# The lower halves of sixteen weight pieces are made by GpSimd and not by VectorE

## The chip, the cores and the metric

The kernel runs on one core of a Trainium2 chip. The metric is the device time of one execution in microseconds (us). The engines of a core work side by side, each through its own list of instructions in a fixed order, and wait for each other through semaphores: TensorE (PE in the profile, PEld for its weight loads), VectorE (DVE), ScalarE (ACT), GpSimd (POOL) and SyncE (SP, which issues most DMAs).

## The reference, cut to what matters

A trunk of two layers over 512 tokens of width 1024 in float32: an RG-LRU block, a gated conv-MLP, an RWKV-7 time-mixing block and a second gated conv-MLP, with an RMS norm ahead of each. The change touches the weights of two of the RWKV block's products:

```
xs_rkv = jnp.stack([h + xx * mix[0], h + xx * mix[1], h + xx * mix[2]])
rkv = jnp.einsum('sbtd,sde->sbte', xs_rkv, w_rkv)
r, k, v = rkv[0], rkv[1], rkv[2]
```

`w_rkv[0]` makes r, `w_rkv[1]` makes k, both 1024 x 1024.

## The kernel before, in words

**Products in three passes.** A float32 product is made of three products of a shorter type. Each operand is split into a higher part `hi`, rounded to that type (F32R), and a lower part `lo = src - hi`; `mm3` (L50) then adds wh*xh, wh*xl and wl*xh in one PSUM bank. In `split` (L92) ScalarE makes `hi` (L94, a CAST in the profile) and VectorE makes `lo` (L97, a TENSOR_TENSOR that reads `src` and `hi` from SBUF).

**Weights stream in pieces.** `plan_weights` (L100) lists all weight pieces of the kernel in the order in which they are used. A piece is 128 partitions x 1024 values, 512 KB. `weights_load` (L161) issues its DMA into a tile `raw`, `weights_split` (L172) makes `wh` and `wl` of it, and `next_weights` (L188) hands out the next piece, with loads 3 pieces ahead and splits 2 (3 in one product) ahead. `raw`, `wh`, `wl` and many other tiles share a ring of 21 buffers (`b4`, L84). k has 8 pieces, r the next 8, then come those of v.

**The stage of the change.** The feed-forward block of the first layer ends at about 540 us of the span. Then come: the small matrices of the decay and the gates (`rwkv_lora_k`, L1036), the k product (blocks 0 to 3 beside that, blocks 4 to 7 in `rwkv_krv`, L1128), the r product, and from `rwkv_chunks` (L1350) the v product with the recurrence. A product is `project_gen` (L197): for an output group of four PSUM banks it takes one piece after the other, the last two together.

**Beside the products** VectorE runs `prepare` (L1162), once for each half of the heads: it scales k and the decay, sums squares through TensorE (`ssq`, L1185; `sst`, L1200), takes reciprocals (tile `n`, L1202 and L1204), which TensorE transposes (`rec`, L1208), VectorE splits (L1211), TensorE spreads (`knb`, L1217) and VectorE multiplies in (L1218). After it `solve` (L1264) inverts 32 x 32 triangles in 31 steps of two instructions each (L1308, L1310) and writes its result XN (L1315), which TensorE's `m1p` (L1334) waits for. The `mix` tiles (L965, L970, L97) are the split operands of r and v.

**GpSimd before** has little to do here: constants (`selk`, `sel`, `n`), the unit matrix X of `solve` (L1303, L1304), the triangle `masks` of the recurrence (L1373, and nine selections at L1380), and small copies (`rts` L1444, `tu` L1447).

**What sets the order.** The program text gives priorities, background work is spread between the products by counts (`background`, L62), and a scheduler of the framework then orders each engine's list by its own estimates, except where `keep_in_program_order` or a dependency fixes it. Once written, an engine's list is strictly in order: an instruction that waits holds all behind it.

Of the kernel before, what the change touches and what calls it, by code (L numbers as in the profile page):

```python
# [7 lines left out]
F32 = mybir.dt.float32  # L8
F32R = mybir.dt.float32r
AF = mybir.ActivationFunctionType  # L10
ALU = mybir.AluOpType
# [33 lines left out]
class Kernel:  # L45
# [43 lines left out]
        t = self.b4(F32R, (2, T), name)  # L89
        return t[:, 0], t[:, 1]  # L90

    def split(self, src, hi, lo, dve=False, pin=False):  # L92

        put = (self.nc.vector.tensor_copy if dve else self.nc.scalar.copy)(hi, src)  # L94
        if pin:
            self.tc.keep_in_program_order(put)
        self.nc.vector.tensor_tensor(lo, src, hi.bitcast(F32), ALU.subtract)  # L97


    def plan_weights(self):  # L100
        I = self.I
        plan = []
        self.quads = []

        def piece(w, r0, c0, k):
            return w[r0 : r0 + k * P, c0 : c0 + D // k].rearrange("(k p) c -> p k c", p=P)

        def add(w, r0, c0, k=2):
            plan.append((piece(w, r0, c0, k), k, False, None))

        def full(w, groups, rows=8):
            for g in groups:
                for k in range(0, rows, 2):
                    add(w, k * P, g * 512)

        def ffn(l):
            up, dn = I["ffn_w_up"][l], I["ffn_w_down"][l]

            def gu(six):


                for n in range(2 * six, 2 * six + 2):
                    self.quads.append(len(plan))
                    a = lambda i, j: piece(up, j * 512, (1 - i) * DFF + n * 256, 4)
                    if n in HALVES:
                        for first, more in (((0, 0), None), ((1, 1), (1, 0)), ((0, 1), None), ((1, 0), (0, 0)), ((1, 1), None)):
                            plan.append((a(*first), 4, True, more and a(*more)))
                    else:
                        for i, j in ((1, 0), (0, 0), (1, 1), (0, 1)):
                            plan.append((a(i, j), 4, False, None))  # L130
                self.quads.append(len(plan))

            def dd(row, n):
                for g in range(2):
                    for k in range(0, n, 2):
                        add(dn, row + k * P, g * 512)

            gu(0)
            for six in range(1, 6):
                gu(six)  # L140
                if six < 5:
                    dd((six - 1) * 512, 4)
            dd(2048, 8)

        full(I["lru_w_in"][0], [2, 3, 0, 1])
        full(I["lru_w_out"][0], [0, 1])
        ffn(0)
        for i in (1, 0):
            full(I["rwkv_w_rkv"][0, i], [0, 1])
        for g in range(4):  # L150
            for k in range(0, 8, 4):
                add(I["rwkv_w_rkv"][0, 2], k * P, g * 256, 4)
        for h in range(2):
            for g in range(4):
                add(I["rwkv_w_out"][0], h * 512, g * 256, 4)
        ffn(1)
        self.plan = plan
        self.loaded, self.splitted = {}, {}
        self.n_load = self.n_split = self.n_used = 0
# [12 lines left out]
    def weights_split(self, upto, pin=False):  # L172
        while self.n_split < min(upto, len(self.plan)):
            i = self.n_split
            if self.plan[i][2]:
                self.n_split += 1
                continue
            self.weights_load(i + 1)
            raw = self.loaded.pop(i)
            k = self.plan[i][1]  # L180
            hi = self.b4(F32R, (k, D // k), f"wh{i}")
            lo = self.b4(F32R, (k, D // k), f"wl{i}")
            for j in range(k) if i == 0 else [slice(0, k)]:
                self.split(raw[:, j], hi[:, j], lo[:, j], pin=pin)
            self.splitted[i] = (hi, lo)
            self.n_split += 1

# [1599 lines left out]
```

## Time and profile before

| | us |
|---|---|
| three runs | 1277.94, 1277.94, 1279.10; median 1277.94 |
| the profiled execution | 1279.1 |
| its span, first to last instruction | 1277.3 |
| VectorE busy in it | 929.2 |
| ScalarE busy in it | 642.8 |
| GpSimd busy in it | 131.1 |

The profiled execution is 1.16 us above the median of the runs; 1.8 us of it lie around the span. TensorE's clock was granted at 0.998 of full speed on average. The profile gives groups of instructions by source line, engine and tiles, the waits between engines, busy time by window, and a timeline in which a row can stand for several instructions of one kind that follow each other (x2, x4); the time of such a row reaches from the start of the first to the end of the last.

### The profile page before, as it was taken

The page shows a single profiled execution, that of the slowest core. Times are in us where ns is not written, and L with a number is a line of the kernel's source. Part 1 is how long each engine was busy: PE and PEld are TensorE (multiplying, and loading weights), DVE is VectorE, ACT ScalarE, POOL GpSimd, SP SyncE. Part 2 cuts the span into 40 slices and gives each one's busy share as a digit, 9 for nine tenths or more (in the row PEclk, how much of TensorE's full clock was granted, in tenths as well). Part 3 has the DMA queues.
Part 4 walks back from the last instruction along what each step waited for, and adds up shares of the span by engine and source line. Part 5 has one row for each costly group of instructions (what it writes and reads, how often), then busy time and mean ns, then how long its engine had stood idle before and what let it go on. Part 6 is the DMA issues. An engine that isn't in the chain of part 4 may idle for free. (4 is left out here: it accounts for less than half of the span.)

```text
span 1277.3 us, 22409 instructions
## 1 busy us (share of the span) xinstructions
PE 1256.0 (98%) x9259; PEld 1067.4 (84%) x9259; DVE 929.2 (73%) x1412; ACT 642.8 (50%) x1006; POOL 131.1 (10%) x206
## 2 busy tenths in 40 slices
PE   9999999999999999999999898999999999999998
PEld 8777888989898989877778797778889898989896
DVE  5998678767676767789999967778776666666654
ACT  6797455434343434559845356545644334343442
POOL 3000001010101010010012145310010101000000
PEclk9999999999999999999999999999999999999999
DMA  7312335445454544413222122122345454545431
GB/s 228 109 53 97 98 119 114 158 106 167 97 175 89 181 83 137 141 57 110 67 75 68 35 63 85 50 94 83 127 88 181 83 182 83 182 83 182 98 133 66
DMA packets 117829, 141.37 MB, mean 111 GB/s; under 512 B 10138, under 2 KB 91748, under 8 KB 117600
## 3 DMA queue, kind: packets, MB, share of 16 engines
q1 hardware_dynamic: 100528, 122.44, 29.9%
q0 software_dynamic: 16624, 16.47, 8.3%
q8 instruction: 72, 1.18, 0.4%
q10 hardware_dynamic: 576, 1.05, 0.2%
q14 instruction: 29, 0.24, 0.1%
HBM read 135.41 MB, written 4.52 MB: 110 GB/s over the span
## 5 line engine op out<-in xcount | busy, mean ns | idle before, releaser
L97 DVE TENSOR_TENSOR wl<-raw,wh 128x1024 fp32r<-128x1024 f32 (+1 forms) x161 | 194.4, 1213 | 123.6 <-ACT wh L94 103.8
L94 ACT CAST wh<-raw 128x1024 fp32r<-128x1024 f32 (+1 forms) x161 | 165.9, 1043 | 179.8 <-PE acc L54 40.7
L54 PE MATMUL accU<-xs,wh 128*128 128x512 f32 x448 | 138.6, 391 | 0.0
L54 PE MATMUL accG<-xs,wh 128*128 128x512 f32 x448 | 138.6, 390 | 0.0
L54 PE MATMUL acc<-hid,wh 128*128 128x512 f32 x384 | 117.9, 389 | 0.0
L748 DVE TENSOR_TENSOR lo<-raw,hi 128x1024 fp32r<-128x1024 f32 x70 | 85.5, 1222 | 39.4 <-PE accU L54 32.0
L747 ACT CAST hi<-raw 128x1024 fp32r<-128x1024 f32 x70 | 73.7, 1054 | 60.4 <-PE accU L54 25.3
L54 PEld LDWEIGHTS accU<-xs,wh 128*128 128x128 f32 x448 | 83.7, 188 | 17.1
L54 PEld LDWEIGHTS accG<-xs,wh 128*128 128x128 f32 x448 | 83.7, 188 | 17.0
L54 PE MATMUL accU<-xs,wl 128*128 128x512 f32 x224 | 87.2, 389 | 0.0
L54 PE MATMUL accG<-xs,wl 128*128 128x512 f32 x224 | 87.2, 389 | 0.0
L54 PE MATMUL accA<-xt,hi 128*128 128x256 f32 x480 | 83.5, 277 | 0.0
L54 PEld LDWEIGHTS acc<-hid,wh 128*128 128x128 f32 x384 | 71.4, 188 | 14.3
L54 PE MATMUL acc<-xs,wh 128*128 128x512 f32 x256 | 80.9, 398 | 0.0
L694 DVE SCALAR_TENSOR_TENSOR cv<-gpad,pv,cv 128x512 f32<-128x512 f32 x96 | 69.1, 747 | 13.1 <-ACT cv L692 12.7
L848 PE MATMUL acc<-wh,hid 128*128 128x512 f32 (+1 forms) x200 | 76.2, 381 | 0.0
L849 PE MATMUL acc<-wl,hid 128*128 128x512 f32 (+1 forms) x200 | 76.1, 381 | 0.0
L847 PE MATMUL acc<-wh,hid 128*128 128x512 f32 (+1 forms) x200 | 76.1, 381 | 0.0
L54 PE MATMUL acc<-hid,wl 128*128 128x512 f32 x192 | 74.3, 389 | 0.0
L168 POOL DMA_DIRECT2D raw<-in_ffn_w_up_dram x20 | 25.7, 1285 | 469.8 <-DVE x L863 166.5
L54 PEld LDWEIGHTS accA<-xt,hi 128*128 128x128 f32 x480 | 72.6, 188 | 0.0
L54 PE MATMUL accA<-xt,lo 128*128 128x256 f32 x240 | 66.3, 276 | 0.0
(411 smaller groups left out, 2938.0 us busy)
## 6 DMA issues: line engine op xcount, KB each, us to landing
raw<-in_ffn_w_up_dram SPq DMA_DIRECT2D x106, 512.0 KB, 3.9
raw<-in_ffn_w_down_dram SPq DMA_DIRECT2D x48, 512.0 KB, 4.0
raw<-in_ffn_w_up_dram POOLq DMA_DIRECT2D x30, 512.0 KB, 5.7
raw<-in_rwkv_w_rkv_dram SPq DMA_DIRECT2D x24, 512.0 KB, 3.8
raw<-in_lru_w_in_dram SPq DMA_DIRECT2D x16, 512.0 KB, 4.0
raw<-in_lru_w_out_dram SPq DMA_DIRECT2D x8, 512.0 KB, 3.8
raw<-in_rwkv_w_out_dram SPq DMA_DIRECT2D x8, 512.0 KB, 3.8
xd<-x SPq DMA_DIRECT2D x8, 256.0 KB, 2.1
```

The lines of the kernel that those rows point to most:

```text
L54: mm = lambda *a, **kw: self.nc.tensor.matmul(ps, *a, skip_group_check=more, **kw)
L94: put = (self.nc.vector.tensor_copy if dve else self.nc.scalar.copy)(hi, src)
L97: self.nc.vector.tensor_tensor(lo, src, hi.bitcast(F32), ALU.subtract)
L168: self.nc.gpsimd.dma_start(raw, more, accum_op=ALU.add)
L694: nc.vector.scalar_tensor_tensor(cv, pair.gp[:, e, j : j + T], cw(j), cv, ALU.mult, ALU.add)
L747: nc.scalar.copy(hi, f[p])
L748: tt(lo, f[p], hi.bitcast(F32), ALU.subtract)
L847: nc.tensor.matmul(ps, hh[:, s], wh[:, k, m], start=kk == 0, stop=False)
L848: nc.tensor.matmul(ps, hl[:, s], wh[:, k, m], start=False, stop=False)
L849: nc.tensor.matmul(ps, hh[:, s], wl[:, k, m], start=False, stop=kk == blocks - 1)
```

## The change

`split` gets a switch `pool`, with which the subtraction for `lo` is issued on GpSimd. `plan_weights` remembers which entries of the plan are the pieces of k and r (`aside`), and `weights_split` sets the switch for them. Sixteen subtractions of 128 x 1024 move; the casts, the loads, the sizes of the tiles and the matmuls stay.

```
-    def split(self, src, hi, lo, dve=False, pin=False):
+    def split(self, src, hi, lo, dve=False, pin=False, pool=False):
...
-        self.nc.vector.tensor_tensor(lo, src, hi.bitcast(F32), ALU.subtract)
+        (self.nc.gpsimd if pool else self.nc.vector).tensor_tensor(lo, src, hi.bitcast(F32), ALU.subtract)
...
         ffn(0)
+        first = len(plan)
         for i in (1, 0):
             full(I["rwkv_w_rkv"][0, i], [0, 1])
+        self.aside = range(first, len(plan))
...
-                self.split(raw[:, j], hi[:, j], lo[:, j], pin=pin)
+                self.split(raw[:, j], hi[:, j], lo[:, j], pin=pin, pool=i in self.aside)
```

Since the scheduler orders the lists anew, other instructions move too. In the changed program the line numbers behind the plan are higher by two (L1204 is L1206 there); the numbers of tiles are the same in both.

GpSimd's list at the end of the stage, before; LT_6284 and X belong to `solve`, tu to the recurrence:

```order
L1303 MEMSET X 128x1024
L1304 AFFINE_SELECT X<-X 128x1024
L1373 MEMSET masks 128x384
L1444 COPY rts<-AR_4906 64x128
L1380 AFFINE_SELECT masks<-masks 64x64 x9
L1444 COPY rts<-AR_4906 64x128 x3
L1409 MEMSET tu 64x256
```

The same place now:

```order
L1306 AFFINE_SELECT X<-X 128x1024
L97 TENSOR_TENSOR wl_5689<-raw_5599,wh_5688 128x1024
L97 TENSOR_TENSOR wl_5695<-raw_5686,wh_5694 128x1024
L97 TENSOR_TENSOR wl_5790<-raw_5692,wh_5789 128x1024
L97 TENSOR_TENSOR wl_5877<-raw_5787,wh_5876 128x1024
L1375 MEMSET masks 128x384
L1446 COPY rts<-AR_4906 64x128
L1382 AFFINE_SELECT masks<-masks 64x64 x9
L1446 COPY rts<-AR_4906 64x128 x3
L97 TENSOR_TENSOR wl_5955<-raw_5874,wh_5954 128x1024
L1411 MEMSET tu 64x256
```

Four pieces of r stand ahead of the masks, and the last piece of r, wl_5955, stands behind the masks, their selections and four copies.

TensorE's list where the last two pieces of r (wh_5876 with wl_5877, and wh_5954 with wl_5955) meet the banks acc_5783 to acc_5786, before:

```order
L54 MATMUL acc_5786<-mix,wh_5876 128x512 x2
L54 MATMUL acc_5786<-mix,wl_5877 128x512
L54 MATMUL acc_5783<-mix,wh_5954 128x512 x2
L54 MATMUL acc_5784<-mix,wh_5954 128x512 x2
L54 MATMUL acc_5785<-mix,wh_5954 128x512 x2
L54 MATMUL acc_5786<-mix,wh_5954 128x512 x2
L54 MATMUL acc_5783<-mix,wl_5955 128x512
L54 MATMUL acc_5783<-mix,wh_5954 128x512 x2
```

And now, from the second half of the knb products on:

```order
L1219 MATMUL knb<-rec,back 128x512 x2
L54 MATMUL acc_5783<-mix,wl_5877 128x512
L1219 MATMUL knb<-rec,back 128x512 x2
L54 MATMUL acc_5783<-mix,wh_5954 128x512 x2
L54 MATMUL acc_5784<-mix,wh_5876 128x512 x2
L54 MATMUL acc_5784<-mix,wl_5877 128x512
L54 MATMUL acc_5783<-mix,wl_5955 128x512
L54 MATMUL acc_5783<-mix,wh_5954 128x512 x2
```

Before, all products with wh_5876 and eight with wh_5954 stood ahead of the first with wl_5955. Now five matmuls stand between the last knb product and the first with wl_5955.

VectorE's list around the second round of reciprocals (tile n_5222; D_5527 and X are the steps of `solve`), before:

```order
L97 TENSOR_TENSOR wl_5877<-raw_5787,wh_5876 128x1024
L1308 TENSOR_TENSOR D_5527<-A,X 128x240
L965 TENSOR_SCALAR mt<-x,om 128x512
L1310 TENSOR_TENSOR X<-X,D_5527 128x20x12
L1202 TENSOR_SCALAR n_5222<-sst 128x4x8
L1308 TENSOR_TENSOR D_5527<-A,X 128x247
L1204 RECIPROCAL n_5222<-n_5222 128x4x8
L1310 TENSOR_TENSOR X<-X,D_5527 128x19x13
L1204 RECIPROCAL n_5222<-n_5222 128x4x8
```

And now:

```order
L1310 TENSOR_TENSOR D_5527<-A,X 128x255
L972 SCALAR_TENSOR_TENSOR mt<-x,pv,mt 128x511
L1312 TENSOR_TENSOR X<-X,D_5527 128x17x15
L1204 TENSOR_SCALAR n_5222<-sst 128x4x8
L1310 TENSOR_TENSOR D_5527<-A,X 128x256
L1206 RECIPROCAL n_5222<-n_5222 128x4x8
L1312 TENSOR_TENSOR X<-X,D_5527 128x16x16
L1206 RECIPROCAL n_5222<-n_5222 128x4x8
```

Three steps of `solve` (D 128x252, 128x255, 128x256 and their updates of X), two instructions of L970 and one of L965 that stood behind the reciprocals stand ahead of them now. Counted over the lists, VectorE has seven pieces fewer from its first L1046 to the end of the first round of reciprocals and is the same there otherwise; six fewer and these nine instructions more from there to the end of the second round; one fewer, and these nine fewer, from there to XN.

## The prediction

> **What bounds the kernel now.** I read the page first, for the engine that is full and for the group that the change touches; then the windows of the stage in which k and r are made; then what TensorE waits for there.
>
> ```profile
> PE 1256.0 (98%) x9259; PEld 1067.4 (84%) x9259; DVE 929.2 (73%) x1412; ACT 642.8 (50%) x1006; POOL 131.1 (10%) x206
> L97 DVE TENSOR_TENSOR wl<-raw,wh 128x1024 fp32r<-128x1024 f32 (+1 forms) x161 | 194.4, 1213 | 123.6 <-ACT wh L94 103.8
> ...
> 576.00:617.00 41.00, 40.12 (x181) 31.22 (x180) 37.96 (x73) 39.31 (x67) 1.00 (x18) 1.00 0.33 99
> 617.00:640.00 23.00, 22.18 (x208) 16.26 (x208) 21.98 (x37) 17.52 (x40) 2.23 (x2) 1.00 0.27 79
> 640.00:672.00 32.00, 31.07 (x138) 23.33 (x139) 31.65 (x69) 13.25 (x21) 4.49 (x14) 1.00 0.22 67
> 672.00:696.00 24.00, 23.25 (x337) 20.91 (x337) 23.55 (x46) 12.38 (x27) 3.53 (x5) 1.00 0.21 67
> ...
> PE m1p L1334 <- DVE XN L1315: 0.7, 1, 0.7
> PE rec L1208 <- DVE n L1204: 0.5, 1, 0.5
> ```
>
> The numbers of a window are its length and then busy PE, PEld, DVE, ACT, POOL. TensorE is full in the whole run, and in this stage VectorE is nearly full too: 37.96 of 41 us, 21.98 of 23, 31.65 of 32, 23.55 of 24. TensorE's idle time here is only 0.88 + 0.82 + 0.93 + 0.75 = 3.38 us. That is all that a lighter VectorE could give back in the stage. The two waits show where VectorE is late already: at the reciprocals (rec) and at the end of the solve (m1p) TensorE waits for it with no slack, so whatever VectorE loses ahead of these points TensorE loses too. GpSimd is nearly idle. The question is whether VectorE gets faster when GpSimd takes the pieces.
>
> **What is taken from VectorE.** The step from a piece to the next instruction:
>
> ```profile
> 584.22 1.20 DVE L97 TENSOR_TENSOR wl<-raw,wh 128x1024 fp32r<-128x1024 f32 x1
> 585.34 1.05 DVE L1107 TENSOR_TENSOR_SCAN AR<-keep,sg 128x128 f32<-128x128 f32 x3
> ...
> 616.12 0.74 DVE L1204 RECIPROCAL n<-n 128x32 f32<-128x32 f32 x2
> ...
> 661.85 0.34 DVE L1204 RECIPROCAL n<-n 128x32 f32<-128x32 f32 x1
> ```
>
> One piece takes 585.34 - 584.22 = 1.12 us out of VectorE's stream. By the lists seven pieces go ahead of the first round of reciprocals, which ends at 616.86 (7 x 1.12 = 7.8 us), and six between it and the end of the second round at 662.19 (6.7 us).
>
> **What a piece costs on GpSimd.** No row shows this subtraction there. The nearest are its product bv, also of two float32 tiles but 512 wide, and its copies:
>
> ```profile
> 740.60 1.04 POOL L1538 TENSOR_TENSOR bv<-x,bon 128x512 f32<-128x512 f32 x1
> 774.15 2.03 POOL L1538 TENSOR_TENSOR bv<-x,bon 128x512 f32<-128x512 f32 x1
> 704.20 0.40 POOL L1447 COPY tu<-x 64x256 f32<-64x256 f32 x1
> 737.55 0.29 POOL L1444 COPY rts<-AR 64x128 f32<-64x128 f32 x1
> 719.04 1.06 POOL L1447 COPY tu<-x 64x256 f32<-64x256 f32 x2 [4.78 <-DVE wl L97]
> ...
> 740.85 0.69 DVE L1431 TENSOR_TENSOR W<-s,masks 128x512 f32<-128x512 f32 x1
> 774.06 1.21 DVE L97 TENSOR_TENSOR wl<-raw,wh 128x1024 fp32r<-128x1024 f32 x1
> 709.99 0.42 DVE L1310 TENSOR_TENSOR X<-X,DA 128x247 f32<-128x247 f32 x1
> 719.23 0.60 DVE L1310 TENSOR_TENSOR X<-X,DA 128x247 f32<-128x247 f32 x1
> ```
>
> bv took 1.04 us at 740.60. Twice the width gives at most 2.08 us. From 128 to 256 elements a copy grows by 0.11 us, so about 0.2 us of an instruction do not grow with its size, and 2 x (1.04 - 0.2) + 0.2 gives 1.9 us. I take **2.0 us** for a piece.
>
> **What that does to VectorE.** These rows also show the two engines in each other's way. Beside L1431, which reads one input from PSUM, bv took 1.04 us. At 774.15, beside an L97 that reads two SBUF tiles and had begun at 774.06, it took 2.03: it stood until L97 was through, and L97 lost nothing (1.21). The other way round, L1310 with two SBUF inputs took 0.60 us while a copy that had begun ahead of it ran on GpSimd, and 0.42 without. So whoever begins second waits. A copy of 0.40 us has about 0.2 us of data, and 0.18 us is what L1310 lost. I take it that a piece of 2.0 us holds back a VectorE instruction that reads two SBUF tiles for **1.85 us**, between its data part of 1.7 and the whole 2.0. Ends: nothing, if VectorE slips in between; 4.06 us, twice the row 2.03, if the waits go both ways. The nearest rows (0.60 against 0.42) speak for a hold, so a piece moved costs VectorE 1.85 and saves it 1.12.
>
> The Trainium skill's page SBUF — State Buffer, section Who interferes with whom, says that a VectorE instruction with two SBUF inputs and a GpSimd instruction that reads SBUF exclude each other for a whole instruction, whichever comes first; by that rule a hold is the full length of a piece, 2.0 and not 1.85, and the sum below 0.15 x 11.8 = 1.8 us higher. Its page GPSIMD Engine Reference, section 3.1 (Elementwise — side-by-side cycle accounting), has 4497 ns for a 2048-wide two-input add on GpSimd; half of that is an estimate of 2.25 us, and the sum would be 0.4 x 11.8 + 0.25 = 5 us higher. No row here shows a hold that long.
>
> **The sum, stretch by stretch.**
>
> ```profile
> L1218 DVE SCALAR_TENSOR_TENSOR AR<-AR,nkk,knb 128x512 f32<-128x512 f32 x7 | 4.9, 742 | 0.1
> L1227 DVE TENSOR_TENSOR AR<-acc,AR 128x512 f32<-128x512 f32 x4 | 2.7, 682 | 0.0
> L1300 DVE STREAM_TRANSPOSE A<-D 128x1024 f32<-128x1024 f32 x1 | 2.0, 1954 | 0.3 <-ACT D L1295 0.3
> L970 DVE SCALAR_TENSOR_TENSOR mt<-x,pv,mt 128x511 f32<-128x511 f32 x10 | 7.3, 742 | 0.0
> L965 DVE TENSOR_SCALAR mt<-x,om 128x512 f32<-128x512 f32 x6 | 2.9, 498 | 0.0
> L1308 DVE TENSOR_TENSOR D<-A,X 128x255 f32<-128x255 f32 x2 | 0.9, 455 | 0.0
> L1310 DVE TENSOR_TENSOR X<-X,D 128x255 f32<-128x255 f32 x2 | 0.8, 420 | 0.0
> ...
> 622.63 1.27 POOL L1304 TENSOR_SCALAR_AFFINE_SELECT X<-X 128x1024 f32<-128x1024 f32 x1
> ...
> 662.54 0.60 PE L1208 MATMUL rec<-ident,n 128*40 128x128 f32 x4
> ```
>
> *To the first reciprocals.* VectorE's work there is by the code almost all on SBUF tiles. -7.8 + 7 x 1.85 = +5.2 us, less the 41 - 37.96 = 3.0 us in which it idled: **+2.1 us** for TensorE, which waits there already. If none of that idle time can be used, +5.2.
>
> *To the second.* The scheduler filled what it thought was freed: two L970, one L965 and three steps of the solve stand ahead now, 2 x 0.74 + 0.50 + 3 x (0.455 + 0.42) = 4.6 us. L1218 and L1227 read PSUM and L1300 has one input: 9.6 us of some 47, so a fifth of the holds falls beside work that does not mind. -6.7 + 4.6 + 0.8 x (6 x 1.85) = +6.8. GpSimd's selection for X, 1.27 us beside L1218 before, comes behind a piece now and lies beside SBUF work: +1.0. Idle there was 1.02 + 0.35 = 1.37, and rec came 0.35 us behind the reciprocals: +6.8 + 1.0 - 1.7 = **+6.1 us**. Here the gain is spent even with no hold: -6.7 + 4.6 leaves 2.1.
>
> *The last piece of r* has a queue of its own:
>
> ```profile
> 663.26 0.43 POOL L1373 MEMSET masks<- 128x384 f32 x1 [39.35 <-PE rec L1208]
> ...
> 667.19 1.05 POOL L1444 COPY rts<-AR 64x128 f32<-64x128 f32 x3
> ...
> 551.50 11.36 PE L54 MATMUL lg<-hx,g 128*128 128x512 f32 x48
> 666.25 0.73 PE L1217 MATMUL knb<-rec,back 40*128 40x512 f32 x2
> 666.91 0.73 PE L54 MATMUL acc<-mix,wh 128*128 128x512 f32 x2
> ```
>
> The masks wait for rec; masks, copies and selections end at 668.24, 5.7 us behind rec (662.54). wl_5955 stands behind them and is there at 5.7 + 2.0 = 7.7. TensorE's last knb product was through at 666.91; five matmuls later, at 11.36 / 48 = 0.24 us a step, it wants wl_5955 at 668.1, 5.5 behind rec: **+2.2 us**. Behind wl_5955 on GpSimd stand the recurrence's memset and copies, whose own inputs come later. The lower end is zero, if the cast that makes wh_5954 is later still.
>
> *From there to XN* VectorE has 4.6 us of moved work and a piece of 1.12 less, against one hold. TensorE, late by then, no longer waits for XN: **-0.7 us**. The loads wait for `raw`, which a later wl frees later; they have slack of more than a piece, and I cost that at nothing. If that cover is gone, ScalarE's casts come late and add up to 2 us.
>
> Sum: 2.1 + 6.1 + 2.2 - 0.7 = **+9.7 us**. Against the profiled execution that is 1279.1 + 9.7 = 1288.8; against the median of the runs, 1.16 us lower, 1277.94 + 9.7 = **1287.6 us**.
>
> **The rivals.**
>
> *Nothing is held* (the two share the reads without loss). VectorE then has 2.1 us to spare or more at each point; TensorE gets back the 0.5 at rec and the 0.7 at m1p and pays 2.2 at wl_5955: +1.0, **1278.9 us**. For it: L1310 lost only 0.18 us. Against it: that was nearly all of the copy's data.
>
> *Faster.* Nothing is held, and wl_5955 comes in time since the casts of r come earlier too: TensorE gets back up to the 3.38 us of the stage, **1274.6 us**. It decides itself at wl_5955: a piece of 2.0 us would have to be there 2.2 us sooner than GpSimd's queue lets it. Little speaks for that.
>
> *GpSimd stands and VectorE runs on.* VectorE, back to back, never lets go for long, and a piece takes 4.06 us. Then the pieces themselves are late:
>
> ```profile
> 582.27 1.05 ACT L94 CAST wh<-raw 128x1024 fp32r<-128x1024 f32 x1
> 585.48 0.50 PE L54 MATMUL acc<-mix,wl 128*128 128x512 f32 x1 [0.33 <-DVE wl L97]
> 642.57 0.50 PE L54 MATMUL acc<-mix,wl 128*128 128x512 f32 x1
> ...
> 639.84 2.95 ACT L94 CAST wh<-raw 128x1024 fp32r<-128x1024 f32 x3
> ```
>
> The cast ready at 583.3 gives wl at 587.4, 1.9 us behind 585.48; the first of the three from 639.84, ready at 640.9, gives it at 645.0, 2.4 behind 642.57; wl_5955 is 4.3 late. 1.9 + 2.4 + 4.3 - 1.2 = +7.4, **1285.3 us**.
>
> That the change does not do what it says is ruled out by the lists: all sixteen stand on GpSimd.
>
> **How the numbers follow.** The hold, my forecast: 0.55. GpSimd standing: 0.18. Nothing held: 0.19. Faster: 0.08. A measurement of this kernel tells some 0.2%, 2.6 us, from no change, so the first two are slower (0.73), the third is the same (0.19). The predicted time is the forecast's, 1287.6. The range takes in nothing held less 1 us, 1277.9, and above that the forecast with its first stretch at +5.2 and each of the 13 holds 0.4 us longer, 1287.6 + 3.1 + 4.7 = 1295.4; I give 1277.5 to 1295.5.
>
> **What would show it.** L97 on GpSimd at 2 us or more; on VectorE, in the stretch from 576 us, L1107 and L1186 to L1192 longer beside pieces by up to 1.8 us; a wait of TensorE for n (L1204, now L1206) of 2 us and then of several, and one for wl on GpSimd of about 2 us late in r; outside 560 to 700 us nothing. Wrong would be a VectorE whose means stay as they are beside GpSimd's pieces, or waits for wl at many places and none for n.

## The result and the profile after

| | before | with the change |
|---|---|---|
| median of four runs each, us | 1278.18 | 1301.31 |
| lowest and highest, us | 1277.94, 1279.1 | 1299.05, 1303.46 |
| profiled execution, its span, us | 1279.1, 1277.3 | 1303.46, 1301.8 |

The ratio is 1.0177, with an interval of 1.0165 to 1.0189: 23.1 us slower. The forecast was 9.7 us slower with a range up to 1295.5, so the time lies 5.8 us above the range. The direction came out, and so did the hold of VectorE; the size did not, and one part of the mechanism, what TensorE's clock does behind a long wait, was missing from the sum.

The page after, the line of busy times and the group of the pieces on VectorE:

```profile
PE 1268.5 (97%) x9259; PEld 1075.7 (83%) x9259; DVE 941.3 (72%) x1396; ACT 643.0 (49%) x1006; POOL 171.3 (13%) x222
L97 DVE TENSOR_TENSOR wl<-raw,wh 128x1024 fp32r<-128x1024 f32 (+1 forms) x145 | 175.0, 1213 | 119.7 <-ACT wh L94 99.7
```

VectorE has sixteen instructions fewer, and its busy time rose from 929.2 to 941.3. Sixteen pieces of 1.21 us should have taken 19.4 off, to 909.8, so its other instructions together became 31.5 us longer: 1.97 us for each piece that left. GpSimd's own share is this row (how long the shortest, the middle and the longest took, in ns, and when the first and the last began):

```profile
L97 POOL TENSOR_TENSOR wl<-raw,wh x16: 2359/2411/3407, 530.3 to 692.4; 128x1024 fp32r<-128x1024 f32 x16
```

A piece takes 2.41 us there, not 2.0. These are the windows after, at the times of the prediction's table (length, then busy PE, PEld, DVE, ACT, POOL, then the granted clock), and TensorE's waits between 560 and 760 us (total, times, longest):

```profile
576.00:617.00 41.00, 38.69 (x173) 30.05 (x172) 38.74 (x61) 34.95 (x58) 17.63 (x24) 1.00 0.29 87
617.00:640.00 23.00, 17.04 (x119) 11.76 (x117) 19.29 (x30) 12.58 (x25) 4.83 (x2) 0.85 0.20 67
640.00:672.00 32.00, 28.06 (x165) 21.69 (x166) 28.80 (x45) 17.57 (x34) 11.65 (x6) 0.89 0.17 50
672.00:696.00 24.00, 19.47 (x66) 12.37 (x65) 20.70 (x39) 6.74 (x12) 9.15 (x16) 0.74 0.18 55
```

```profile
PE rec L1210 <- DVE n L1206: 8.7, 2, 4.4
PE acc L54 <- ACT wh L94: 4.1, 2, 3.3
PE acc L54 <- POOL wl L97: 2.1, 3, 1.2
```

The wait for n (L1204 before, L1206 now) grew from 0.5 us to 8.7, as forecast, and that for XN is gone. Two things in the windows were not forecast: VectorE, though held, has more idle time than before in the last three of them, and TensorE's clock, 1.00 in all four windows before, is 0.85, 0.89 and 0.74 in these three.

### Where the 23 us went

The first windows below are of the kernel before: the whole stage, from the first L1046 to the end of XN, and the two stretches of the prediction. Then the same work after.

```profile
566.63:694.97 128.34, 125.11 (x848) 98.51 (x846) 123.38 (x243) 87.50 (x161) 14.02 (x55) 1.00 0.25 77
566.63:616.86 50.23, 49.49 (x222) 38.90 (x220) 47.09 (x94) 45.13 (x75) 4.75 (x35) 1.00 0.29 87
616.86:662.19 45.33, 43.43 (x305) 32.66 (x306) 44.05 (x86) 26.41 (x52) 2.23 (x2) 1.00 0.19 59
```

```profile
567.89:719.21 151.32, 134.57 (x830) 103.22 (x829) 135.97 (x229) 86.25 (x154) 49.88 (x69) 0.91 0.22 67
567.89:626.04 58.15, 50.02 (x222) 38.79 (x220) 54.73 (x88) 47.81 (x79) 26.25 (x43) 0.99 0.25 78
626.04:684.15 58.11, 49.87 (x306) 36.69 (x306) 52.25 (x89) 24.17 (x46) 14.28 (x7) 0.88 0.15 46
```

The stage took 151.32 - 128.34 = 23.0 us longer. TensorE's idle time in it went from 128.34 - 125.11 = 3.2 to 151.32 - 134.57 = 16.8 us, which is 13.5 more. The other 9.5 us are in its busy time (125.11 to 134.57), for the same matmuls: TensorE itself was slower. The stage began 1.3 us later; two pieces are made ahead of it.

That VectorE is held is seen best in the small steps of `solve`. This is VectorE after (start, duration), and then GpSimd at that time:

```profile
655.34 1.89 DVE L1310 TENSOR_TENSOR D<-A,X 128x31 f32<-128x31 f32 x1
657.26 2.32 DVE L1312 TENSOR_TENSOR X<-X,D 128x31 f32<-128x31 f32 x1
659.62 2.30 DVE L1310 TENSOR_TENSOR D<-A,X 128x60 f32<-128x60 f32 x1
661.95 0.22 DVE L1312 TENSOR_TENSOR X<-X,D 128x60 f32<-128x60 f32 x1
```

```profile
654.79 7.05 POOL L97 TENSOR_TENSOR wl<-raw,wh 128x1024 fp32r<-128x1024 f32 x3 [4.63 <-ACT wh L94]
```

Three pieces run on GpSimd from 654.79 to 661.84, and VectorE does just three instructions meanwhile, one beside each. The fourth, which comes behind the last piece, takes 0.22 us. The two engines take turns, instruction by instruction, and a step of 0.2 us pays for a whole piece.

Why TensorE was slower is in its own timeline after (an idle time ahead of a row stands in brackets at its end) and in three windows:

```profile
626.19 1.01 PE L1210 MATMUL rec<-ident,n 128*40 128x128 f32 x4 [4.42 <-DVE n L1206]
654.76 1.21 PE L54 MATMUL acc<-mix,wh 128*128 128x512 f32 x4 [3.33 <-ACT wh L94]
684.29 1.01 PE L1210 MATMUL rec<-ident,n 128*40 128x128 f32 x4 [4.30 <-DVE n L1206]
```

```profile
626.04:632.00 5.96, 5.81 (x16) 4.60 (x17) 5.45 (x10) 2.00 (x5) 0.00 (x0) 0.50 0.00 0
656.00:663.00 7.00, 6.39 (x16) 4.53 (x16) 6.79 (x7) 2.56 (x4) 5.84 (x3) 0.51 0.01 2
684.15:697.00 12.85, 12.47 (x28) 7.86 (x29) 8.61 (x15) 4.58 (x9) 6.51 (x15) 0.50 0.34 102
```

Behind each of the three long waits the granted clock is 0.50 for 6 to 13 us. These windows hold 5.81 + 6.39 + 12.47 = 24.7 us of matmuls. At half the clock that would be up to 12 us lost; the busy time says 9.5.

The second of these waits is not one for VectorE itself, but for ScalarE's cast. TensorE waited at that place before too, 1.57 us. The cast stands in ScalarE's list behind `fac` (L1179), and `fac` waited for VectorE's BK, 2.48 us now and 1.38 before; the instruction ahead of that BK took 2.26 us beside a piece:

```profile
649.12 0.82 ACT L1179 ACTIVATE fac<-BK,oka,pv 128x512 f32<-128x512 f32 x1 [2.48 <-DVE BK L1194]
```

So VectorE's lateness also reached TensorE by way of ScalarE's list.

### The profile page after: what moved, and what is told of

Same layout as the page of the kernel before. It is cut to its first block, busy times and chain, and to the rows that moved or that the text cites. A ratio compares the mean times of both kernels' runs of the same rounds, so it can differ in the third digit from the quotient of the medians.

```text
span 1301.8 us, 22427 instructions
## 1 busy us (share of the span) xinstructions
PE 1268.5 (97%) x9259; PEld 1075.7 (83%) x9259; DVE 941.3 (72%) x1396; ACT 643.0 (49%) x1006; POOL 171.3 (13%) x222
## 3 DMA queue, kind: packets, MB, share of 16 engines
q10 hardware_dynamic: 576, 1.05, 0.2%
## 4 chain that ended last, share of the span: by engine, by line
PE 44%; DVE 7%; ACT 2%; issue 1%; POOL 1%; POOLq 0%; DVEq 0%; ACTq 0%
PE accU L54 6%; PE accG L54 6%; PE acc L54 5%; PE accA L54 4%; PE acc L850 3%; PE acc L851 3%; PE acc L849 3%; PE accF L54 2%; DVE X L1312 1%; PE accD L54 1%; PE acc L1258 1%; PE s L1426 1%; PE acc L1259 1%; PE acc L1260 1%; PE pd L1508 1%
## 5 line engine op out<-in xcount | busy, mean ns | idle before, releaser
L97 DVE TENSOR_TENSOR wl<-raw,wh 128x1024 fp32r<-128x1024 f32 (+1 forms) x145 | 175.0, 1213 | 119.7 <-ACT wh L94 99.7
L54 PE MATMUL acc<-mix,wh 128*128 128x512 f32 x192 | 66.3, 429 | 4.1 <-ACT wh L94 4.1
```

Of the source, the lines that this page charges most:

```text
L54: mm = lambda *a, **kw: self.nc.tensor.matmul(ps, *a, skip_group_check=more, **kw)
L97: (self.nc.gpsimd if pool else self.nc.vector).tensor_tensor(lo, src, hi.bitcast(F32), ALU.subtract)
```

## Experiments

The theory after the result, T1: a piece on GpSimd holds VectorE for its length because both read SBUF; VectorE comes late to the reciprocals; TensorE waits there, and its clock falls behind each long wait. The rivals: the order of the work or GpSimd's queue costs the time, without a hold; the clock falls for another reason. Before is 1278.2 to 1279.1 us in each group of runs. The column "longer" is VectorE's busy time over the 929.2 of before, less 1.21 us for each piece that it no longer makes. The diffs are against the changed kernel; those of e7_late, e9_late_busy and e12_bits are against the kernel before.

| run | median, us | ratio to before, interval | VectorE busy | longer |
|---|---|---|---|---|
| the change | 1301.31 | 1.0177, 1.0165 to 1.0189 | 941.3 | 31.5 |
| e2_write | 1277.23 | 0.9987, 0.9978 to 0.9997 | 915.1 | 5.3 |
| e5_read | 1312.25 | 1.0269, 1.0252 to 1.0286 | 960.0 | 30.8 |
| e6_write | 1283.75 | 1.0039, 1.0024 to 1.0054 | 933.4 | 4.2 |
| e8_copy | 1300.95 | 1.0177, 1.0162 to 1.0193 | 952.0 | 22.8 |
| e10_half | 1296.35 | 1.0141, 1.0126 to 1.0156 | 937.7 | 27.9 |
| e3_k | 1282.87 | 1.0035, 1.0021 to 1.005 | 933.6 | 14.1 |
| e4_r | 1295.09 | 1.013, 1.0115 to 1.0146 | 938.0 | 18.5 |
| e7_late | 1301.22 | 1.0176, 1.0161 to 1.0192 | 929.2 | 0.0 |
| e1_busy | 1306.68 | 1.0217, 1.0201 to 1.0232 | 942.6 | 32.8 |
| e9_late_busy | 1308.14 | 1.0233, 1.0216 to 1.025 | 931.2 | 2.0 |
| e12_bits | 1301.84 | 1.0175, 1.0158 to 1.0192 | 931.9 | 2.7 |

### Is it the reading? GpSimd writes only (e2_write)

```diff
+        if pool:
+            self.nc.gpsimd.memset(lo.bitcast(F32), 0.0)
+            self.nc.gpsimd.memset(lo.bitcast(F32), 0.0)
+            return
-        (self.nc.gpsimd if pool else self.nc.vector).tensor_tensor(lo, src, hi.bitcast(F32), ALU.subtract)
+        self.nc.vector.tensor_tensor(lo, src, hi.bitcast(F32), ALU.subtract)
```

> The lower bits of k's and r's weights are left out (set to zero): on GpSimd two memsets of the tile stand in the place of the subtraction, so GpSimd is about as long at it but reads nothing. T1 (the hold is one of reading): no VectorE instruction is longer than without GpSimd work, TensorE's waits for n are under 1 us, 1278 (1275 to 1283), near the kernel before. Rival (the order of the work, GpSimd's queue or the semaphores cost the time): 1288 or more. Rival (GpSimd's writes hold VectorE as its reads do): some 1297 to 1302.

1277.23 us. GpSimd is at a tile for 1.9 us (two memsets of 0.96 us), against 2.41 for a piece, VectorE is rid of the sixteen pieces, and TensorE no longer waits for n at all. This run is 24 us under the change. It does not differ in the reading alone: the memsets are shorter, need neither `raw` nor the cast, and the lists are ordered a little differently. The next three runs hold these things nearer to equal. The run shows a second thing: with VectorE relieved of all sixteen and held by nothing, the kernel is 1.7 us faster than the 1278.92 of its own group. So little is what there was to win.

### The same work beside VectorE's, reading and not (e5_read, e6_write, e8_copy)

Here VectorE keeps all pieces, and GpSimd does something to the same tile behind it, so nothing is taken off VectorE:

```diff
+        self.nc.vector.tensor_tensor(lo, src, hi.bitcast(F32), ALU.subtract)
+        if pool:                                   # e5_read
+            self.nc.gpsimd.tensor_tensor(lo, src, hi.bitcast(F32), ALU.subtract)
+        if pool:                                   # e6_write, two of these
+            self.nc.gpsimd.memset(lo.bitcast(F32), 0.0)
+        if pool:                                   # e8_copy, two of these
+            self.nc.gpsimd.tensor_copy(lo, lo.bitcast(F32))
```

> Nothing is left out: VectorE makes all pieces as in the kernel before, and GpSimd makes the sixteen of k and r once more into the same tile behind it. T1: holds of 2.2 us for thirteen pieces and nothing saved: first stretch 7 x 2.2 - 3.0 = +12.4, second 0.8 x 6 x 2.2 - 1.4 = +9.2, and clock lost after the waits as in the changed kernel, +12: some 1310 (1302 to 1320). Rival (no hold; pieces late and lists changed): 1278 to 1288.

> The lower bits of k's and r's weights are left out: as the kernel with the double work, but behind VectorE's subtraction GpSimd sets the tile to zero twice, with the same waits and about the same time on GpSimd, and reads nothing. T1: no hold; the pieces come up to 2 us later, 1281 (1277 to 1288), at least 15 us under the kernel with the double reading. Rival (order, queue or semaphores): within 5 us of that kernel.

> Nothing is left out: as the kernel in which GpSimd sets the tile to zero twice behind VectorE's subtraction (1283.75), with the same order on TensorE and VectorE, but GpSimd copies the tile onto itself twice, some 1.06 us each by the 128x256 copy of 0.40, so it reads one tensor. T1 (any reading of SBUF by GpSimd holds VectorE for the length of the instruction): VectorE's small steps take up to 1 us beside a copy, each copy holds one instruction 0.9 us: 1295 to 1310. Rival (only GpSimd's two-input instructions hold it): within 3 us of that kernel, 1281 to 1287.

1312.25, 1283.75 and 1300.95 us, all three inside what T1 gave. The last two have the same order of work on VectorE and ScalarE, and on TensorE up to a few neighbouring matmuls of the recurrence; the one sets the tile to zero and the other reads it (and writes it again), for about the same time on GpSimd, and that is 17.2 us. These are the first steps of `solve` in the two, e6_write and then e8_copy, with GpSimd's copies of the latter last:

```profile
645.97 0.19 DVE L1313 TENSOR_TENSOR D<-A,X 128x31 f32<-128x31 f32 x1
646.19 0.22 DVE L1315 TENSOR_TENSOR X<-X,D 128x31 f32<-128x31 f32 x1
646.44 0.22 DVE L1313 TENSOR_TENSOR D<-A,X 128x60 f32<-128x60 f32 x1
```

```profile
656.49 0.20 DVE L1313 TENSOR_TENSOR D<-A,X 128x31 f32<-128x31 f32 x1
656.72 1.08 DVE L1315 TENSOR_TENSOR X<-X,D 128x31 f32<-128x31 f32 x1
657.84 1.07 DVE L1313 TENSOR_TENSOR D<-A,X 128x60 f32<-128x60 f32 x1
```

```profile
656.70 1.04 POOL L99 CAST wl<-wl 128x1024 fp32r<-128x1024 f32 x1 [5.79 <-DVE D L1313]
657.80 1.04 POOL L100 CAST wl<-wl 128x1024 fp32r<-128x1024 f32 x1
```

Beside memsets (646.16 to 648.12 in e6_write) the steps keep their 0.2 us; beside a copy of 1.04 us they take 1.08 and 1.07; beside a piece 2.3. The hold is the length of what GpSimd reads, with one input or two. So the rivals of order, queue and semaphores fall.

### Does a finer grain help? (e10_half)

```diff
+        for k in range(2) if pool else ():
+            self.nc.gpsimd.tensor_tensor(lo[:, k], src[:, k], hi[:, k].bitcast(F32), ALU.subtract)
+        if not pool:
+            self.nc.vector.tensor_tensor(lo, src, hi.bitcast(F32), ALU.subtract)
```

> Nothing is left out: the changed kernel with each piece as two instructions of 128x512 on GpSimd. T1 (the two engines take turns instruction by instruction, so GpSimd's whole reading time is lost to VectorE whatever its grain): VectorE's busy time within 5 us of the 941.3 of the changed kernel, single holds of about 1.1 us, and a time of 1296 to 1308. Rival (what counts is the length of one hold): half the loss, 1292 or less.

1296.35 us: 5 us better than whole pieces, and still 18 behind. VectorE in `solve`:

```profile
651.03 1.23 DVE L1315 TENSOR_TENSOR X<-X,D 128x31 f32<-128x31 f32 x1
652.29 1.21 DVE L1313 TENSOR_TENSOR D<-A,X 128x60 f32<-128x60 f32 x1
653.53 1.20 DVE L1315 TENSOR_TENSOR X<-X,D 128x60 f32<-128x60 f32 x1
```

Each hold is half as long and there are twice as many (27.9 us in all against 31.5), as T1 has it for engines that take turns. The time lies at the lower end of what was expected: TensorE's busy time is 1263.4 us here and 1268.5 in the changed kernel, so most of the gain is in TensorE's own speed.

### Which pieces? (e3_k, e4_r)

```diff
-        self.aside = range(first, len(plan))
+        self.aside = range(first, first + 8)            # e3_k
+        self.aside = range(first + 8, len(plan))        # e4_r
```

> Nothing is left out: only the eight pieces of k are on GpSimd. T1: the loss up to the first reciprocals (+9.2) and the lower clock behind that wait (some 3.4) stay, the second stretch goes as before: some 1291 (1287 to 1294), one long wait for n. Rival (the loss comes only where both queue up): 1284 or less.

> Nothing is left out: only the eight pieces of r are on GpSimd. T1: nothing lost to the first reciprocals; the second stretch and the clock behind its waits cost what is left of the 23 us: some 1290 (1286 to 1294), the long wait for n only at the second. Rival (the second stretch is late only because the first was): 1284 or less.

1282.87 and 1295.09 us: 4.7 and 16.9 over before, 21.6 together, against 23.1 for both at once. The costs nearly add up, but not in the halves that I expected: k's time is the one that the rival gave, and r's is 1 us above T1's range. For k alone neither the long wait nor the lower clock came; with r alone there was a long wait at the first reciprocals already, because the first piece of r (on GpSimd at 612.4 us) lies ahead of them. The waits of TensorE, e3_k first:

```profile
PE rec L1210 <- DVE n L1206: 1.2, 1, 1.2
```

```profile
PE rec L1210 <- DVE n L1206: 6.9, 2, 3.9
PE acc L54 <- ACT wh L94: 3.3, 1, 3.3
```

k's pieces make the first rec 5.6 us later (622.6 us against 617.0), in several waits of which none exceeds 1.6 us, and the clock is 1.00 in every window of e3_k. With r the waits are of 3 and 4 us, and the clock in the windows from 617 us on is 0.93, 0.93 and 0.87.

### Is it the wait that lowers the clock? (e7_late, e1_busy, e9_late_busy, e12_bits)

In e7_late VectorE makes all pieces, and the reciprocals are made late by a chain of small multiplications on GpSimd:

```diff
+            for d in range(24):
+                nc.gpsimd.tensor_scalar(n8[:, :, 0:8], n8[:, :, 0:8], 1.0, None, ALU.mult)
```

> Nothing is left out and VectorE makes all pieces, as in the kernel before; ahead of each rec the reciprocals go through 24 multiplications by 1 on GpSimd (128x32 each, some 0.2 us), so that TensorE waits for n some 3 to 5 us twice, with no piece on GpSimd. T1 (a wait of that length by itself lowers TensorE's clock for the work behind it): matmuls behind each wait at half the clock for 4 us or more, windows of 6 us behind the waits at 0.8 or less, and the time higher by the waits and about as much again, some 1293 (1288 to 1300). Rival (the clock is lowered by something else in the changed kernel): no window under 0.95 and only the waits' length more, 1284 to 1288.

1301.22 us, 1.2 us above T1's range. The waits were longer than meant (8.8 and 6.2 us: a multiplication took 0.29 us, some of them up to 1.05), and VectorE's busy time stayed at the 929.2 us of before. The windows of e7_late:

```profile
617.00:640.00 23.00, 14.20 (x71) 9.22 (x69) 14.24 (x26) 7.35 (x16) 11.51 (x26) 0.70 0.13 46
630.00:636.00 6.00, 6.00 (x14) 3.83 (x14) 4.83 (x8) 3.74 (x7) 2.23 (x2) 0.50 0.27 87
690.00:696.00 6.00, 6.00 (x21) 4.18 (x20) 4.35 (x8) 3.52 (x8) 3.14 (x11) 0.79 0.64 194
```

The half clock is there without a single piece on GpSimd. TensorE's busy time in the whole run is 1265.1 us against 1256.0 before, for the same matmuls: 9.1 us of the 22.7 by which the span grew are TensorE's own slowness, the rest is waiting.

The other three were to take the long wait away. e1_busy puts forty idle transposes ahead of each rec in the changed kernel, e9_late_busy sixty in e7_late; e12_bits cuts e7_late's chain into six parts with a few transposes and useful matmuls between:

```diff
+            for d in range(40):                          # e1_busy; range(60) in e9_late_busy
+                self.tc.keep_in_program_order(nc.tensor.transpose(pr[:, d % 4 * P : d % 4 * P + P], self.ident, self.ident))
...
+            for d in range(6):                           # e12_bits
+                for e in range(3):
+                    nc.gpsimd.tensor_scalar(n8[:, :, 0:8], n8[:, :, 0:8], 1.0, None, ALU.mult)
+                for c in range(8 if d < 5 else 4):
+                    self.tc.keep_in_program_order(nc.tensor.transpose(pr[0:40, c % 4 * P : (c % 4 + 1) * P], n8[:, c % 4, :], self.ident))
```

> Nothing is left out: the changed kernel with forty more 128x128 transposes of the identity ahead of each of the two groups of rec, so that TensorE has some 4 us of idle work where it waited 4.4 and 4.3 us for n. T1 (VectorE is held, and TensorE's clock falls after each long wait): the waits for n shrink to under 1 us, the granted clock of 617 to 640 us and 672 to 696 us rises from 0.85 and 0.74 to 0.95 or more and 0.85 or more, and the time falls by about 8 us to some 1293 (1289 to 1297). Rival (the clock falls for another reason, such as the work itself): windows as before, 1299 to 1304. Rival (no clock effect is worth anything): the same time within 2 us although the wait is gone.

> Nothing is left out: as the kernel with the late reciprocals (1301.22), with sixty more 128x128 transposes of the identity ahead of each rec, some 6.5 us of idle work in place of most of each wait. T1 (the wait itself lowers the clock, and the clock costs time): no half clock behind rec, windows of 6 us at 0.9 or more there, and the time lower by the clock's part, some 7 us: 1294 (1290 to 1297). Rival (the clock behind a wait costs nothing, or isn't due to the wait): within 2 us, 1299 or more.

> Nothing is left out: VectorE makes all pieces; ahead of each rec the reciprocals go through 18 multiplications by 1 on GpSimd in six groups of three, and behind each group TensorE transposes them (8 small matmuls, the last group 4), with useful matmuls between, so that TensorE is about as late at knb as in the kernel with the late reciprocals, but its wait is in six parts of about 1 us and no long one. T1 (one long wait lowers the clock): no window behind rec under 0.95, and the time higher by the parts of the wait and the extra transposes alone (2 x 4.4 us of these and some 2 x 3 of waits): 1293 (1286 to 1296). Rival (what lowers the clock is GpSimd's work or late data, not one long wait): windows of 0.5 to 0.8 as there, 1299 or more.

1306.68, 1308.14 and 1301.84 us; no time came out as T1 had it. By the time alone, e9_late_busy and e12_bits lie where their rivals were put (1299 or more), and e1_busy lies above T1 and both rivals. The added transposes cost time themselves (they keep TensorE busy 4.8 us a round in e1_busy and 6.7 in e9_late_busy), and the long waits were not taken away, so these three times decide nothing; the clock records do. In e1_busy the wait moved behind rec: TensorE now waited 2.89 and 3.35 us at knb, for VectorE, and the half clock moved there with it. In e9_late_busy rec stood earlier in TensorE's list than in e7_late, and 5.7 and 4.5 us of waiting were left behind the transposes. In e12_bits the first of the six waits of the first round was still 2.98 us; its waits for n add up to 11.1 us, not 6, and the clock fell once more later in that round, with no wait above 0.9 us there. In its second round, though, no wait exceeded 1.85 us, TensorE was idle for 5.7 of the 18 us of these rows, and the clock stayed:

```profile
678.00:684.00 6.00, 3.67 (x20) 2.42 (x18) 5.97 (x17) 0.00 (x0) 3.23 (x5) 1.00 0.00 1
684.00:690.00 6.00, 3.67 (x24) 2.58 (x25) 5.22 (x13) 0.00 (x0) 2.83 (x8) 1.00 0.01 3
690.00:696.00 6.00, 4.92 (x31) 3.63 (x30) 0.31 (x1) 0.92 (x2) 2.43 (x8) 1.00 0.00 0
```

All thirteen profiles together say it more plainly. These are TensorE's waits of 1.2 us or more between 560 and 760 us, from the timelines, and the mean granted clock of the 3 us behind each:

| length of the wait | number | clock behind it |
|---|---|---|
| 1.20 to 1.60 us | 20 | 1.00 behind 19, 0.73 behind one (1.36 us, in e7_late) |
| 1.85 to 2.98 us | 17 | 0.50 to 0.70 behind 12, 1.00 behind 5 |
| 3.09 to 8.80 us | 19 | 0.50 to 0.76 behind all |

They are waits for VectorE, ScalarE and GpSimd alike, in kernels with held instructions and without. That a long wait is followed by a lower clock is shown. What decides in the middle group can be read from the same traces. In each of the thirteen, the times at which the clock falls or rises lie whole multiples of 3.41 us apart. Cut the stretch from 560 to 760 us into frames of that length along these times, and take the frames that ran at the full clock: of 32 in which TensorE was busy for less than 1.6 us, 31 are followed by a frame at 0.50; of 658 in which it was busy for longer, three are. So it is not the length of the wait alone, but how much idle time falls into one frame. In e4_r a wait of 2.10 us, up to 670.45, lies in one frame, and the next frame is at 0.50; in e8_copy one of 2.41 us, up to 653.47, is spread over two, and the clock stays (e4_r first; the number behind the length is TensorE's busy time, the clock stands third from the end):

```profile
667.83:671.24 3.41, 1.31 (x9) 0.85 (x8) 3.41 (x7) 2.15 (x3) 1.32 (x1) 1.00 0.00 0
671.24:674.65 3.41, 3.06 (x8) 1.85 (x6) 3.41 (x6) 0.00 (x0) 1.30 (x1) 0.50 0.00 0
```

```profile
648.37:651.78 3.41, 2.68 (x12) 1.88 (x10) 3.41 (x5) 3.29 (x10) 2.46 (x3) 1.00 0.31 71
651.78:655.19 3.41, 1.72 (x8) 1.43 (x9) 3.41 (x5) 3.36 (x5) 0.00 (x0) 1.00 0.21 83
655.19:658.60 3.41, 1.74 (x8) 1.13 (x6) 3.34 (x5) 0.13 (x1) 1.84 (x2) 1.00 0.00 0
```

This was found in the traces afterwards; no run set a wait on purpose against the frames. Four frames do not fit: the clock fell after frames with TensorE busy for 1.82 us (e10_half), 2.06 (e7_late, with the wait of 1.36) and 2.49 (e12_bits, the later fall), and it stayed after one with 1.56 us (e12_bits, second round). Why these differ is open. A kernel that keeps the wait and loses only the clock's fall was not found, so the 9.5 us are an account from busy times, not a difference of two runs.

The Trainium skill, page TensorE: Matmul & The Clock Gate, Part 1: The HAM clock gate, says that the clock goes to half after an idle window of some 3.4 us, counted by a window that runs freely. The frames of 3.41 us and the waits above 3.4 us agree with it; that the window has to be idle does not, since the clock fell after frames in which TensorE had worked, such as the one with 1.31 us above.

## Why the prediction was right in kind and wrong in size

What failed are two steps of the sum. It took 3.0 and 1.4 us of VectorE's idle time as cover for the holds, and that time did not shrink; and it put TensorE's speed behind the waits at full, a term at nothing without a reason, where TensorE's matmuls took 9.5 us longer. Stretch by stretch the prediction had +2.1, +6.1 and, from there to XN, 2.2 - 0.7 = +1.5 us; measured were +7.9, +12.8 and (719.21 - 684.15) - (694.97 - 662.19) = +2.3, together 23.0.

- **What holds VectorE**: right. A piece on GpSimd holds the next VectorE instruction on SBUF tiles; by e6_write and e8_copy it is the reading, and e2_write agrees. The Trainium skill's page SBUF — State Buffer, section Who interferes with whom, that the prediction set beside its own count, gave the length better: a hold is the whole piece. The trace agrees, with 2.32 us beside pieces of 2.41. And the prediction's restriction to two SBUF inputs was too narrow. This group has one, here before and after:

```profile
L1189 DVE COPY AR<-ppad 128x512 f32<-128x512 f32 x4 | 1.7, 419 | 0.0
```

```profile
L1191 DVE COPY AR<-ppad 128x512 f32<-128x512 f32 x4 | 4.9, 1230 | 0.0
```

- **The length of a piece**, 2.0 us: mis-sized, 2.41. Doubling the product's row of 1.04 was too little.
- **To the first reciprocals, +2.1**: it was 58.15 - 50.23 = +7.9. VectorE's L97 instructions fell from 13.56 to 5.02 us there (predicted -7.8 for the seven pieces, measured -8.5, as a piece is busy for 1.21 us and not for the 1.12 of its step). The rest of its work grew by (54.73 - 5.02) - (47.09 - 13.56) = 16.2, where 7 x 1.85 = 13.0 was put: GpSimd made eight pieces in this stretch and not seven, at 2.0 us of holds each. The other half of the error is the credit "less the 41 - 37.96 = 3.0 us in which it idled": VectorE's idle time was 50.23 - 47.09 = 3.1 before and 58.15 - 54.73 = 3.4 after. It idled because inputs came late, and they still do. The bound of +5.2 without that credit was nearer.
- **To the second, +6.1**: it was 58.11 - 45.33 = +12.8. The L97 instructions fell from 12.44 to 5.31 us, and the rest of VectorE's work grew by (52.25 - 5.31) - (44.05 - 12.44) = 15.3, of which 4.6 is the work that was moved ahead; -7.1 + 15.3 is 8.2, against -6.7 + 4.6 + 8.9 + 1.0 = 7.8 in the prediction. That was right. The step that failed is the last: VectorE's idle time did not shrink by 1.7 but grew by (58.11 - 52.25) - (45.33 - 44.05) = 4.6. Its waits in the stretch are one of 2.6 us for the knb products, which stood behind matmuls at half the clock, and two of 1.7 and 1.0 us for ScalarE; the waits in this stretch before were 0.6 and 0.3.
- **TensorE's speed**: not in the sum at all. The prediction had a delay of 2 us at the first rec and of 8 by the second, and took the work behind them at full speed. The busy times put this at 9.5 us: 0.5 in the first stretch, 6.4 in the second and 2.5 from there to XN. These are not on top of the differences of the stretches, they are the part of them that is TensorE's own slowness.
- **Late casts**: the prediction had ScalarE's casts late only if the loads were, and put that at nothing. They came late for another reason, `fac` ahead of them, and TensorE's wait there grew from 1.57 to 3.33 us.
- **The last piece of r, +2.2**: wrong. TensorE waited 0.23 us for it, as the second of these rows of after shows. What the piece itself waited for was not GpSimd's queue of masks, which was through 2.36 us earlier, but TensorE's knb products, which were late and slow:

```profile
692.41 2.37 POOL L97 TENSOR_TENSOR wl<-raw,wh 128x1024 fp32r<-128x1024 f32 x1 [2.36 <-PE knb L1219]
694.83 0.79 PE L54 MATMUL acc<-mix,wl 128*128 128x512 f32 x1 [0.23 <-POOL wl L97]
```

- **XN, -0.7**: right, that wait is gone.
- **The upper end of the range**: 13 holds of 0.4 us more are 5.2 and not 4.7, which is what the 11.8 holds of the sum give. Either way the end lies below the measured time.
- **Nothing is held, 1278.9**: that rival was worth having. It is near e2_write, 1277.23, in which GpSimd reads nothing: the price was about right, and the condition was false for pieces that are read.

## What to carry to other kernels

Moving work to GpSimd relieves VectorE only if that work doesn't read SBUF while VectorE does: here 1.21 us were taken off and 1.97 put on for each piece, so ask first how long GpSimd reads, and then what VectorE would have done meanwhile. Before a gain is credited, see what the engine's idle time waits for, since idle time that waits for inputs pays for nothing. And where waits leave TensorE idle for more than about half of a stretch of 3.4 us, count the matmuls of at least the next 3.4 us at half the clock; here a wait of 3.1 us or more always did that, and one of 1.9 to 3.0 us in 12 of 17 cases.

## What the runs showed that I had not expected

An instruction of 31 elements a partition (0.20 us) took 2.32 us beside GpSimd's subtraction. TensorE's granted clock fell to 0.50 for 6 to 13 us behind a wait of 3.3 to 4.4 us, in a kernel that keeps TensorE busy 97% of the time; behind 19 of 20 waits of 1.2 to 1.6 us it was 1.00. And GpSimd's memset beside VectorE cost next to nothing: 4.2 to 5.3 us of VectorE's time for 32 memsets of 0.96 us each.
